# Three projection units instead of two in the staged beginning of a hybrid SSD/Conformer layer, with its first loads and casts in another order

## The chip, the cores and the metric

The kernel runs on one core of a Trainium2 chip, in one launch. Time is device time in microseconds (us): the median of several runs of the same program. The engines are named as in the profile: PE (TensorE, the matrix engine; PEld is its weight load), DVE (VectorE), ACT (ScalarE), POOL (GpSimd) and SP (SyncE, which here issues every DMA). All data are float32; the large products use the type fp32r, which PE runs at one pass.

## What is computed

One layer of a diffusion backbone, for 512 latent tokens (L) and 128 context tokens (C), 640 columns in all (T), with a model width of 1024 (eight blocks of 128, KD). Cut to what the beginning computes:

```python
mod = jax.nn.silu(cond) @ prm["w_ada"] + prm["b_ada"]
sh1, sc1, g1, sh2, sc2, g2 = [m[:, None, :] for m in jnp.split(mod, 6, axis=-1)]
h = rms_norm(x, prm["norm_mix_pre"]) * (1 + sc1) + sh1
proj = h @ prm["w_in"]
z, xbc, dt_raw, cf_in = jnp.split(proj, [...], axis=-1)
xbc = jax.nn.silu(dwconv1d(xbc, prm["w_ssd_conv"], prm["b_ssd_conv"]))
xs, b_mat, c_mat = jnp.split(xbc, [...], axis=-1)
# SSD scan forward and backward over chunks of 128 tokens with dt, a, xs, b_mat, c_mat
cf_a, cf_g = jnp.split(cf_in, 2, axis=-1)
u = dwconv1d(cf_a * jax.nn.sigmoid(cf_g), prm["w_cf_conv"], prm["b_cf_conv"])   # 31 taps
# then layer norm, output projection, residual, gated ConvFFN, residual
```

The modulation (`cond @ w_ada`) differs between latent and context tokens, so two rows of it are computed.

## The kernel before, in words

**Layout.** Features lie on the 128 partitions, tokens along the free axis. x is eight tiles of 128 x 640 (T0 to T7). A *unit* is a projection's weight block: 128 output features, 1024 x 128 weights, a DMA of 512 KB. To keep float32 accuracy each weight and each h is split into a high and a low part: ACT copies to fp32r (L165 for weights, L253 for h), then POOL (L167) or DVE (L255) subtracts. A product is then three matmuls (high by high, high by low, low by high), each in two column parts of 384 and 256, so one k block of a unit is six matmuls and a whole unit 48 (`mm3`, L268).

**Weight buffers.** `fetch` (L133) loads raw units into tag `wr`, which has two buffers; `split_unit` splits them into `wh` and `wl`, which have three each. `get_unit(i)` fetches up to two units ahead. A third raw unit can be loaded only when the splits of the first are done with its buffer.

**Beginning.** SP issues the loads: the condition vectors, x, constants, the first block of modulation weights (`load_ada(0)`, eight DMAs of 256 KB, tag order at L97), all parameters (`prms`, 920 columns), the root table `ids` (a repeated 32 x 32 identity), the dt weights `wdts`. ACT computes Silu of the condition (L345), a one-element square root to have its table loaded (L347), and the squares of x (L351); PE sums them over features (`colsum`, L326); ACT and DVE take the reciprocal root (L340, L341); PE spreads it to all partitions (`spread`, L334).

**Staged part (L365 to L396).** The units in `FIRST`, g0 and a0 (gate and value of the Conformer branch), go on by stages rather than one after the other. x is multiplied by the spread root: four tiles on DVE straight from PSUM (L373) and four on POOL (L375) from a copy that ACT makes (L370). Then, for each of four stages s: `ada_first` multiplies one 2 MB block of modulation weights (L294; SP loads blocks 1 to 3 at L367), turns the result (L276) and adds its bias (L285); DVE forms the scale (L380, L381), applies scale and shift to x blocks 2s and 2s+1 (L385); ACT and DVE split them (L253, L255); PE does the dt product (L360) and the two blocks of every unit in `FIRST`.

**After it.** `gate` (L700, Tanh) and `gated` (L705) make the Conformer input; `dtprep` (L448 on) the dt and decay tables, beginning with a cast of `ids` (L452), a transposing product (L458), and using the exponential of `a_log` (L479); `conv31` the 31-tap convolution, one DVE instruction a tap (L721), accumulating in PSUM tile P2, its first step on ACT (L718). Then the list `seq` is worked through: units B0, C0, xs0, g1, ... each with `proj` (PSUM tiles P0 and P1 in turn) and its consumer; for B0 and C0 that is `conv3_silu` (L417 on ACT, L419 and L421 on DVE, L428 Silu). `ssd` builds decays for each head pair and casts selectors from `ids` (L608). Four steps scale parameters by 0.5 on POOL (L771, L773).

**Order.** The program is built with `schedule_with_timeline_sim=True`. Each engine's instruction order is then not the order of the Python text: a planner simulates a timeline and gives each engine, of the instructions that are ready in its model, the one that is first in the text; `tc.high_priority(offset=-3000)` puts `conv31` behind the rest. `tc.issue_after(ins)` adds an order edge: what it encloses is queued behind `ins` on the engine of `ins`. Once built, each engine runs its queue strictly in order.

Of the kernel before, what the change touches and what calls it, by code (L numbers as in the profile page):

```python
# [7 lines left out]
F32 = mybir.dt.float32  # L8
F32R = mybir.dt.float32r
AF = mybir.ActivationFunctionType  # L10
# [3 lines left out]
P = 128  # L14
# [3 lines left out]
T = L + C  # L18
# [29 lines left out]
def hybrid_layer_kernel(ctx: ExitStack, tc: tile.TileContext, xT, ct, prm, cst, wrest, wdt, idhl_d, wada1, wada2, win,  # L48
# [51 lines left out]

    load_ada(0)
    prms = sb.tile([P, NPRM], F32, tag="prms", name="prms")
    sy.dma_start(prms, prm)
    ids = sb.tile([P, 32], F32, tag="idhl", name="ids")
    sy.dma_start(ids, idhl_d)
    wdts = sb.tile([P, KD, 32], F32, tag="DTW", name="wdts")
    sy.dma_start(wdts, wdt)
    ones = sb.tile([P, 1], F32, tag="ones", name="ones")
# [37 lines left out]
    def get_unit(i):  # L146
        fetch(i + AHEAD)
        return ready.pop(i)
# [29 lines left out]
    IN_INDEX = _in_index()  # L178
    FIRST = ("g0", "a0")
    plan_in(*FIRST)  # L180
    seq = []

    def s_proj(*names):
        for n in names:
            plan_in(n)
            seq.append(("proj", n))

    s_proj("B0", "C0")
    seq += [("btok", 0), ("cb", 0)]
# [57 lines left out]

    split_ins = [None]
    EARLY = 16

    def split_act(hi_tag, lo_tag, src, lo_eng):
        hi = slot(hi_tag, F32R)
        ac.activation(hi, src, AF.Copy)  # L253
        lo = slot(lo_tag, F32R)
        split_ins[0] = lo_eng.tensor_tensor(lo, src, hi.bitcast(F32), SUB)  # L255
        return hi, lo
# [87 lines left out]

    ac.activation(cts, cts, AF.Silu)  # L345

    ac.activation(sb.tile([P, 1], F32, tag="warm", name="warm"), epsc, AF.Sqrt)  # L347
    pst = psq(1)
# [15 lines left out]
    h_hi, h_lo = [], []  # L364
    firsts = [(get_unit(unit_of[n][0]), psum((0, 2, 1)[i])) for i, n in enumerate(FIRST)]  # L365
    for s in range(1, 4):
        load_ada(s)  # L367
    ada_first(0)
    rs0 = slot("S12")
    ac.activation(rs0, prs[:, 192:192 + T], AF.Copy)  # L370
    for k in range(KD):
        if k < 4:
            ve.tensor_tensor(xs_[k], xs_[k], prs[:, 192:192 + T], MUL)  # L373
        else:
            gp.tensor_tensor(xs_[k], xs_[k], rs0, MUL)  # L375
    for s in range(4):
# [37 lines left out]
    def conv3_silu(pt, i, out):  # L414
# [12 lines left out]
        else:  # L427
            ac.activation(out, out, AF.Silu)  # L428

    ACM = DT = acHL = WD = CDs = idr = None  # L430
    cT = [None, None]
# [16 lines left out]
    def dtprep():  # L448

        nonlocal ACM, DT, acHL, WD, CDs, idr  # L450
        idr = sb.tile([P, 32], F32R, tag="idr", name="idr")
        ve.tensor_copy(idr, ids)  # L452
        raw = slot("T8")
# [24 lines left out]
        aexp = sb.tile([P, 32], F32, tag="aexp", name="aexp")  # L478
        ac.activation(aexp, prm_col("a_log", 0, 32), AF.Exp)  # L479
        ve.scalar_tensor_tensor(by(e), DT, -1.0, aexp.unsqueeze(1).to_broadcast([P, NCH, 32]), MUL, MUL)  # L480
# [111 lines left out]
    def ssd(p):  # L592
# [12 lines left out]
        def decays():  # L605
            peas = []
            sel = sm.tile([P, 2, 2, 64], F32R, tag="sel", name=nm("sel"), bufs=1)
            ve.tensor_copy(sel, ids.rearrange("p (d h) -> p d h", d=2)[:, :, 2 * p:2 * p + 2]  # L608
                           .unsqueeze(3).to_broadcast([P, 2, 2, 64]))
            for d in range(2):  # L610
                pea = psq(d)
                te.matmul(pea[:, 0:L], sel[:, d].rearrange("p h q -> p (h q)"), acHL[:, 0:L], start=True, stop=True)
                ea.append(slot(f"S{10 + d}"))
                peas.append(pea)
            for o, pea in zip(ea, peas):
                ac.activation(o[:, 0:L], pea[:, 0:L], AF.Exp)
# [157 lines left out]
    gate(0, firsts[0][1])  # L774
    gated(0, firsts[1][1])
    dtprep()
    conv31(0)
# [684 lines left out]
```

## Time and profile before

| | |
|---|---|
| Median of 3 runs | 1012.25 us (1012.11 to 1014.71) |
| Profiled execution, its own time | 1010.71 us |
| Span of its instructions | 1008.9 us |
| Mean granted PE clock over the span | 0.993 |
| HBM read / written | 97.87 MB / 3.67 MB |
| Chain that ended last, shares | PE 81%, DVE 7%, ACT 5%, POOL 3%, issue 2%, DMA 2% |

How to read the lines quoted below. A *timeline* row is: start in us from the span's beginning, time in us until the end of the last of the merged instructions, engine, line of the kernel, operation, output tile <- input tiles, shapes, count; in brackets how long the engine was idle before it and what released it ("issue": nothing that the profile shows). Matmul counts are hardware instructions: a float32 product outside fp32r takes two. Matmul ends are modelled, so a row's time can overlap the next one's start. A *windows* row is: the stretch, its length, then busy us and instruction count of PE, PEld, DVE, ACT and POOL, the granted PE clock (1.00 is full), the busy share of the DMA engines and GB/s. A *waits* row is: engine and line, what it waited for, us in total, times, longest. A row of *DMA issues* ends with KB each and the median us from issue to landing. SPq is SP's queue of DMA issues.

### The profile page before, as it was taken

What the parts mean: (1) busy time and instruction counts of PE and PEld (TensorE: products, weight loads), DVE (VectorE), ACT (ScalarE), POOL (GpSimd) and SP (SyncE); (2) the same over time, 40 slices, a digit from 0 to 9 for tenths busy, and PEclk for the clock granted to TensorE, in tenths of its full rate; (3) what the DMA queues carried; (4) which work ended last, traced back from release to release, by engine and by line L of the source; (5) the groups of instructions that cost most, each with busy time, mean ns of one, the idle gap of its engine ahead of it and who ended that gap; (6) DMA issues with size and microseconds to landing.
All of it is one profiled execution on the core that took longest, in us unless ns stands there. A gap on an engine that the chain in (4) does not pass through costs nothing.

```text
span 1008.9 us, 18834 instructions
## 1 busy us (share of the span) xinstructions
PE 968.3 (96%) x7655; PEld 933.7 (93%) x7655; DVE 736.1 (73%) x1093; ACT 457.9 (45%) x766; POOL 588.8 (58%) x426
## 2 busy tenths in 40 slices
PE   4999999999999989999989999999999999999995
PEld 2789999999999978899979999999999999999995
DVE  3789999989999998672286798998988988400004
ACT  6244556674553856842364754233233236322211
POOL 2333877888887896443473696454454456543444
PEclk9999999999999999999999999999999999999998
DMA  9622121122212111559463422222222222222212
GB/s 345 229 80 79 53 94 63 54 74 64 74 43 66 41 50 41 167 165 391 156 206 106 147 84 64 85 70 77 85 71 76 84 70 68 79 79 74 79 37 105
DMA packets 42934, 102.76 MB, mean 102 GB/s; under 512 B 4832, under 2 KB 12768, under 8 KB 42848
## 3 DMA queue, kind: packets, MB, share of 16 engines
q1 hardware_dynamic: 42848, 101.56, 30.4%
q8 instruction: 60, 0.98, 0.4%
q14 instruction: 26, 0.21, 0.1%
HBM read 97.87 MB, written 3.67 MB: 101 GB/s over the span
## 4 chain that ended last, share of the span: by engine, by line
PE 81%; DVE 7%; ACT 5%; POOL 3%; issue 2%; DMA 2%; SPq 0%; POOLq 0%; ACTq 0%; DVEq 0%
PE ps L268 67%; PE ps L1112 3%; PE pq L268 2%; POOL wl L167 2%; PE pq L313 2%; PE pq L666 1%; DVE T L760 1%; ACT wh L165 1%; DVE ps L721 1%; PE pq L655 1%; PE pq L573 1%; DMA wr<-in_wout 1%; PE pq L294 1%; PE pq L631 1%; DMA T<-in_xT 1%
## 5 line engine op out<-in xcount | busy, mean ns | idle before, releaser
L167 POOL TENSOR_TENSOR wl<-wr,wh 128x1024 fp32r<-128x1024 f32 (+3 forms) x127 | 291.7, 2297 | 293.3 <-ACT wh L165 287.4
L268 PE MATMUL ps<-H,wh 128*128 128x384 f32 (+1 forms) x1636 | 322.1, 310 | 4.9 <-DVE M L421 2.2
L165 ACT ACTIVATE wh<-wr 128x1024 fp32r<-128x1024 f32 (+3 forms) x131 | 131.7, 1006 | 342.6 <-PE ps L268 196.8
L268 PE MATMUL ps<-T,wh 128*128 128x384 f32 (+1 forms) x1472 | 273.1, 306 | 1.9 <-ACT S L1080 1.9
L268 PEld LDWEIGHTS ps<-H,wh 128*128 128x128 f32 x1636 | 249.0, 188 | 9.1 <-issue 4.5
L1090 DVE SCALAR_TENSOR_TENSOR S<-ps,prms,S 128x441 f32<-128x441 f32 (+2 forms) x336 | 233.4, 695 | 29.7 <-ACT S L1080 19.2
L268 PEld LDWEIGHTS ps<-T,wh 128*128 128x128 f32 x1472 | 219.3, 188 | 2.3 <-ACT S L1080 2.2
L721 DVE SCALAR_TENSOR_TENSOR ps<-u,prms,ps 128x655 f32<-128x655 f32 x223 | 200.7, 900 | 9.9 <-ACT ps L718 5.4
L268 PE MATMUL ps<-H,wl 128*128 128x384 f32 (+1 forms) x818 | 194.8, 310 | 0.0
L268 PE MATMUL ps<-T,wl 128*128 128x384 f32 (+1 forms) x736 | 166.7, 306 | 0.0
L268 PEld LDWEIGHTS ps<-H,wl 128*128 128x128 f32 x818 | 128.8, 188 | 1.6 <-issue 1.2
L268 PEld LDWEIGHTS ps<-T,wl 128*128 128x128 f32 x736 | 113.0, 188 | 0.0
L341 DVE RECIPROCAL rsm<-rsm 128x160 f32<-128x160 f32 (+2 forms) x9 | 7.3, 815 | 141.5 <-ACT rsm L340 141.5
L268 PE MATMUL ps<-S,wh 128*128 128x384 f32 (+1 forms) x420 | 87.5, 312 | 1.7 <-DVE M L923 1.2
L268 PEld LDWEIGHTS ps<-S,wh 128*128 128x128 f32 x420 | 65.9, 188 | 4.3 <-issue 2.5
L268 PE MATMUL ps<-S,wl 128*128 128x384 f32 (+1 forms) x210 | 54.4, 308 | 0.3 <-POOL wl L167 0.3
L637 ACT ACTIVATE S<-pq,ACM 128x128 f32<-128x128 f32 x140 | 40.9, 372 | 18.3 <-PE pq L631 18.1
L1080 ACT ACTIVATE S<-ps,prms 128x640 f32<-128x640 f32 x42 | 36.5, 868 | 0.0
L268 PEld LDWEIGHTS ps<-S,wl 128*128 128x128 f32 x210 | 35.0, 188 | 0.5 <-POOL wl L167 0.5
L588 POOL TENSOR_TENSOR S<-S,stmp 128x128 f32<-128x128 f32 x36 | 18.6, 517 | 15.1 <-ACT S L577 11.2
L1193 POOL TENSOR_TENSOR H<-S,S 128x640 f32<-128x640 f32 x16 | 25.2, 1578 | 0.0
L648 POOL TENSOR_TENSOR S<-S,M 128x640 f32<-128x640 f32 x14 | 22.1, 1577 | 4.4 <-ACT S L645 4.4
(353 smaller groups left out, 1276.7 us busy)
## 6 DMA issues: line engine op xcount, KB each, us to landing
wr<-in_wup SPq DMA_DIRECT2D x44, 512.0 KB, 3.4
wr<-in_win SPq DMA_DIRECT2D x36, 512.0 KB, 3.5
T<-in_wada SPq DMA_DIRECT2D x49, 256.0 KB, 5.4
wr<-in_wdown SPq DMA_DIRECT2D x16, 512.0 KB, 3.4
wr<-in_wout SPq DMA_DIRECT2D x13, 512.0 KB, 3.4
H<-in_wada SPq DMA_DIRECT2D x23, 256.0 KB, 5.5
S<-in_wada SPq DMA_DIRECT2D x16, 256.0 KB, 5.9
wr<-in_wdown SPq DMA_DIRECT2D x8, 384.0 KB, 3.1
```

The source lines that it names most:

```text
L165: ac.activation(hi[:, :n], raw[:, :n], AF.Copy)
L167: lo_eng.tensor_tensor(lo[:, :n], raw[:, :n], hi[:, :n].bitcast(F32), SUB)
L268: last_mm[0] = te.matmul(out, w, x[:, c0:c1], start=first and i == 0, stop=last and i == 2)
L313: te.matmul(pt[32 * j:32 * j + 32, 0:P], cts[:, kc, :], w[:, j * P:(j + 1) * P], start=kc == 0, stop=kc == KD - 1, tile_position=(0, 32 * j))
L588: gp.tensor_tensor(now, now, tmp, ADD)
L637: ac.activation(r[:, c * P:(c + 1) * P], pb[:, (c - c0) * P:(c - c0 + 1) * P], AF.Relu, scale=-1.0, bias=ACM[:, c, row:row + 1])
L648: (ve if i % 2 or last else gp).tensor_tensor(r, r, cbm[g][d], MUL)
L721: ve.scalar_tensor_tensor(acc, u[:, j:j + UO], w(j), acc, MUL, ADD)
L1080: ac.activation(out, v, AF.Identity, bias=prm_col("ffn_b", i), scale=w(1, 1))
L1090: ve.scalar_tensor_tensor(ob, vl[:, r0 + a - 1:r1 + a - 1, q0 + b - 1:q1 + b - 1], w(a, b), ob, MUL, ADD)
L1112: te.matmul(pt[:, o:o + c1 - c0], w[k] if i in (1, 2) else w[:, k * P:(k + 1) * P], x[:, c0:c1], start=k == 0 and j == 0, stop=k == KD - 1 ...
L1193: gp.tensor_tensor(f_raw[q], a, b, MUL)
```

## The change

- `FIRST` gets a third unit: g0, a0 and B0 go by stages. B0 leaves `seq`; its PSUM tile is P1, and since `proj` goes on alternating from P0, C0 now takes P0, xs0 P1 and so on. B0's convolution `conv3_silu` is written behind `gated(0)` and ahead of `dtprep`. In the text its weights are taken with `get_unit` behind the scaling of x.
- Loads: behind the first modulation block come only the first 56 columns of `prms` (modulation bias and the first norm's gain), then g0 and a0, then `wdts`, the second modulation block, the other 864 columns of `prms`, `ids`, and the other two modulation blocks.
- x is scaled on DVE alone, all eight tiles from PSUM; ACT's copy L370 is gone.
- ACT's one-element square root is queued behind the Silu of the condition, not ahead of it.
- Queued later: the cast of `ids` behind the last low split of h on DVE, the selector cast of `decays` behind that cast, the exponential of `a_log` behind the last high split of h on ACT.

PE's products, the weight splits and the bytes loaded stay the same; the one `prms` load becomes two.

```diff
     load_ada(0)
+
     prms = sb.tile([P, NPRM], F32, tag="prms", name="prms")
-    sy.dma_start(prms, prm)
-    ids = sb.tile([P, 32], F32, tag="idhl", name="ids")
-    sy.dma_start(ids, idhl_d)
-    wdts = sb.tile([P, KD, 32], F32, tag="DTW", name="wdts")
-    sy.dma_start(wdts, wdt)
+    NEAR = _COLS["g_mix_pre"][1]
+    sy.dma_start(prms[:, 0:NEAR], prm[:, 0:NEAR])
...
-    FIRST = ("g0", "a0")
+    FIRST = ("g0", "a0", "B0")
...
-    s_proj("B0", "C0")
+    s_proj("C0")
...
-        ac.activation(hi, src, AF.Copy)
+        hi_ins[0] = ac.activation(hi, src, AF.Copy)
...
-    ac.activation(cts, cts, AF.Silu)
-
-    ac.activation(sb.tile([P, 1], F32, tag="warm", name="warm"), epsc, AF.Sqrt)
+    cond = ac.activation(cts, cts, AF.Silu)
+
+    with tc.issue_after(cond.ins):
+        ac.activation(sb.tile([P, 1], F32, tag="warm", name="warm"), epsc, AF.Sqrt)
...
-    firsts = [(get_unit(unit_of[n][0]), psum((0, 2, 1)[i])) for i, n in enumerate(FIRST)]
-    for s in range(1, 4):
+    firsts = [(get_unit(unit_of[n][0]), psum((0, 2)[i])) for i, n in enumerate(FIRST[:2])]
+    wdts = sb.tile([P, KD, 32], F32, tag="DTW", name="wdts")
+    sy.dma_start(wdts, wdt)
+    load_ada(1)
+    sy.dma_start(prms[:, NEAR:], prm[:, NEAR:])
+    ids = sb.tile([P, 32], F32, tag="idhl", name="ids")
+    sy.dma_start(ids, idhl_d)
+    for s in range(2, 4):
         load_ada(s)
     ada_first(0)
-    rs0 = slot("S12")
-    ac.activation(rs0, prs[:, 192:192 + T], AF.Copy)
     for k in range(KD):
-        if k < 4:
-            ve.tensor_tensor(xs_[k], xs_[k], prs[:, 192:192 + T], MUL)
-        else:
-            gp.tensor_tensor(xs_[k], xs_[k], rs0, MUL)
+        ve.tensor_tensor(xs_[k], xs_[k], prs[:, 192:192 + T], MUL)
+    firsts.append((get_unit(unit_of[FIRST[2]][0]), psum(1)))
...
-        ve.tensor_copy(idr, ids)
+        with tc.issue_after(split_ins[0].ins):
+            late = ve.tensor_copy(idr, ids)
+        first_cast.append(late)
...
-        ac.activation(aexp, prm_col("a_log", 0, 32), AF.Exp)
+        with tc.issue_after(hi_ins[0].ins):
+            ac.activation(aexp, prm_col("a_log", 0, 32), AF.Exp)
...
-            ve.tensor_copy(sel, ids.rearrange("p (d h) -> p d h", d=2)[:, :, 2 * p:2 * p + 2]
-                           .unsqueeze(3).to_broadcast([P, 2, 2, 64]))
+            with tc.issue_after(first_cast[0].ins):
+                ve.tensor_copy(sel, ids.rearrange("p (d h) -> p d h", d=2)[:, :, 2 * p:2 * p + 2]
+                               .unsqueeze(3).to_broadcast([P, 2, 2, 64]))
...
     gate(0, firsts[0][1])
     gated(0, firsts[1][1])
+    bT[0] = slot("M2")
+    conv3_silu(firsts[2][1], 8, bT[0])
     dtprep()
```

More of the change, by code (lines that the diff above doesn't have):

```diff
@@ L248, in hybrid_layer_kernel @@
     split_ins = [None]
+    hi_ins = [None]
     EARLY = 16
@@ L428, in conv3_silu @@
             ac.activation(out, out, AF.Silu)
+    first_cast = []
     ACM = DT = acHL = WD = CDs = idr = None
```

## The prediction, made before the changed kernel was built

> **What bounds the kernel now.** I read the page first, then the windows of the first 75 us and of the long middle, then the timeline of each engine at the beginning, then the waits.
>
> ```profile
> PE 968.3 (96%) x7655; PEld 933.7 (93%) x7655; DVE 736.1 (73%) x1093; ACT 457.9 (45%) x766; POOL 588.8 (58%) x426
> 20.00:25.00 5.00, 0.33 (x1) 0.14 (x1) 4.93 (x10) 2.37 (x4) 5.00 (x6) 0.79 1.05 392
> 25.00:35.00 10.00, 9.37 (x92) 6.50 (x93) 7.48 (x6) 1.75 (x3) 6.79 (x5) 0.76 1.05 387
> 35.00:50.00 15.00, 14.16 (x204) 11.74 (x204) 11.23 (x28) 4.92 (x8) 2.77 (x2) 1.00 0.35 128
> 75.00:80.00 5.00, 5.00 (x36) 5.00 (x34) 4.34 (x9) 1.91 (x3) 2.33 (x1) 1.00 0.31 99
> ```
>
> PE is busy for 968.3 of 1008.9 us, and the change adds no matmul and takes none away. So the time can fall only where PE stands idle or runs at a low clock: about 40 us in all. At the beginning that is the stretch 20 to 25 us (0.33 of 5 us busy), the low clock in 25 to 35 us (0.76 of full speed), and 0.84 us in 35 to 50. A full-clock stretch runs 36 products in 5 us, 0.139 us each: one unit of 48 products costs PE 6.7 us, a quarter of it (one stage) 1.7 us.
>
> The PE timeline says what it waits for:
>
> ```profile
> 9.09 4.08 PE L326 MATMUL pq<-S,ones 128*32 128x160 f32 x40 [1.35 <-ACT S L351]
> 15.31 2.50 PE L334 MATMUL ps<-rsm,csts 128*128 128x160 f32 x8 [0.54 <-DVE rsm L341]
> 17.74 2.13 PE L294 MATMUL pq<-T,cts 128*32 128x128 f32 x40
> 20.31 0.33 PE L276 MATMUL pq<-csts,adar 128*128 128x128 f32 x1 [0.44 <-ACT adar L297]
> 25.63 1.03 PE L360 MATMUL pq<-T,wdts 128*32 128x512 f32 x1 [4.99 <-issue]
> 42.20 1.52 PE L294 MATMUL pq<-T,cts 128*32 128x128 f32 x48
> 71.94 0.84 PE L268 MATMUL ps<-H,wh 128*128 128x384 f32 x4 [2.25 <-DVE M L421]
> ```
>
> After the transpose of the first modulation (L276) PE stands still for 4.99 us until the first dt product (L360), which needs x scaled and shifted. And at 71.94 the unit xs0 has waited 2.25 us for L421: B0's convolution on DVE still reads the PSUM tile that xs0 is to fill.
>
> **The change, part by part.** First what leads to that first dt product.
>
> ```profile
> 12.38 1.28 ACT L340 ACT_TABLE_LOAD   x1
> 13.67 0.39 ACT L340 ACTIVATE rsm<-pq,epsc 128x160 f32<-128x160 f32 x1
> 18.58 3.01 DVE L373 TENSOR_TENSOR T<-T,ps 128x640 f32<-128x640 f32 x4 [3.33 <-ACT S L370]
> 21.65 1.69 DVE L608 CAST sel<-ids 128x256 fp32r<-128x256 f32 x1
> 23.26 0.21 DVE L285 TENSOR_TENSOR modv<-pq,prms 128x4 f32<-128x4 f32 x2
> 23.44 1.31 DVE L380 TENSOR_SCALAR asc<-modv 128x4 f32<-128x4 f32 x1
> 35.52 0.17 DVE L380 TENSOR_SCALAR asc<-modv 128x4 f32<-128x4 f32 x1
> 24.98 1.65 DVE L385 TENSOR_SCALAR T<-T,asc,modv 128x512 f32<-128x512 f32 x4
> 18.63 6.10 POOL L375 TENSOR_TENSOR T<-T,S 128x640 f32<-128x640 f32 x4 [17.39 <-ACT S L370]
> ```
>
> *Square-root table.* The root's table is loaded first and thrown out by Silu, so L340 loads it again at 12.38. Behind Silu it stays in. But the root also needs the column sums, which end at 13.17 (9.09 + 4.08). So the step comes at 13.2 and not 13.67: 0.5 us, not 1.28; the range is 0.3 to 1.28. The Trainium skill, "ScalarE: Activation LUTs", section "What ACT_TABLE_LOAD costs", gives about 2.66 us a switch, 1.28 of it the load and the rest a drain. Here the load takes 1.28 us and the root follows 0.01 us behind it, so no drain stands in the trace; by the page's sum the step would still be held by the column sums.
>
> *Scaling.* DVE began 0.77 us after the spread had ended (15.31 + 2.50 = 17.81), since it waited for ACT's copy L370. The copy is gone. The scaling then starts at about 17.3 and takes 8 x 0.75 (3.01 / 4) = 6.0 us on DVE, to 23.3; the two modv additions (0.21) bring it to 23.5. Now L380 begins at 23.44, since two casts (L452, L608; 1.69 us for the larger) are in the way; they go behind the last split. These parts cancel: +0.1 us. What remains is L380's own length: 1.31 us here and 0.17 in a later stage. It ended when POOL's L375 ended (18.63 + 6.10 = 24.73), so it waited for POOL. Without L375, POOL is free for the splits of g0 and a0, which then run in this same stretch. If L380 falls between two of them the step gains 1.1 us; if it falls at the start of one it loses up to 1.3 (a split is 2.41 us, below). I take -0.4 together with the table.
>
> *Weights ahead of most parameters.* The queue's rows:
>
> ```profile
> 12.75 0.33 SPq L103 DMA_DIRECT2D prms<-in_prm  x1
> 14.77 1.01 SPq L141 DMA_DIRECT2D wr<-in_win  x2
> 16.11 6.13 SPq L98 DMA_DIRECT2D S<-in_wada  x8
> 34.83 48.47 SPq L141 DMA_DIRECT2D wr<-in_win  x8
> 20.65 1.06 ACT L165 ACTIVATE wh<-wr 128x1024 fp32r<-128x1024 f32 x1 [0.40 <-DMA wr<-in_win]
> 26.53 5.26 POOL L167 TENSOR_TENSOR wl<-wr,wh 128x1024 fp32r<-128x1024 f32 x2
> 46.44 2.41 POOL L167 TENSOR_TENSOR wl<-wr,wh 128x1024 fp32r<-128x1024 f32 x1 [2.71 <-ACT wh L165]
> 26.59 5.88 DVE L255 TENSOR_TENSOR H<-T,H 128x640 fp32r<-128x640 f32 x2
> 37.54 1.56 DVE L255 TENSOR_TENSOR H<-T,H 128x640 fp32r<-128x640 f32 x2
> ```
>
> Three issues (parameters, root table, dt weights) stood ahead of the weights. The parameters become 56 of 920 columns, the dt weights come right behind g0 and a0, and the rest of the parameters and the table behind the second ada block. The queues moved 392 GB/s in 20 to 25 us, so 0.59 MB less (864 columns of 512 B, the table's 16 KB, the dt weights' 128 KB) ahead of g0 brings it 1.5 us earlier, and the second ada block about 1.2 us (the dt weights still stand ahead of that one). That block's products (64 records; 48 took 1.52 us at full clock, so 2.03 us) now run behind 25.63. With their data earlier and the scaling on DVE longer, more of them should be planned into the 4.99 us gap: I take 40 of 64, -1.2 us, with 0 and -2.0 as ends.
>
> *Splits.* POOL's two weight splits began only at 26.53, behind the scaling. DVE's two splits of h took 5.88 us beside them and 1.56 alone: PE got the low halves of stage 0 late. Now the weight splits end at about 25 (weights at 19.1, then 1.06 and two times 2.41), before DVE's. PE's loss there: 92 records in 9.37 us, where 24 products (3.3), 64 ada records (2.0) and four dt records (0.9 together, under the 1.03 of the first, since they overlap) make 6.2 at full clock, and the clock of 0.76 explains 2.4; 0.8 is left. I take -0.8 (0 to -0.8).
>
> *Three units by stages.* B0 moves 12 products (1.7 us) into each stage. In 35 to 50 us PE idles 0.84 us, which this can fill: -0.4 (0 to -0.8). The real gain is at 71.94:
>
> ```profile
> 64.15 0.87 ACT L417 ACTIVATE M<-ps,prms 128x640 f32<-128x640 f32 x1
> 68.84 0.99 DVE L419 SCALAR_TENSOR_TENSOR M<-ps,prms,M 128x511 f32<-128x511 f32 x2
> 70.80 0.99 DVE L421 SCALAR_TENSOR_TENSOR M<-ps,prms,M 128x511 f32<-128x511 f32 x2
> 71.87 1.28 ACT L428 ACT_TABLE_LOAD   x1 [6.85 <-DVE M L421]
> 55.61 0.89 DVE L705 SCALAR_TENSOR_TENSOR u<-u,ps 128x512 f32<-128x512 f32 x2 [3.80 <-ACT u L700]
> ```
>
> B0's convolution stands between the dt chain and the taps of the first long convolution and is done only at 71.8. In the changed kernel it is written ahead of both, and PSUM tile 1 (B0's) is needed by xs0 only after the whole of C0, 6.7 us later. Its own work is 0.87 + 0.99 + 0.99 us. So the wait of 2.25 us goes: -2.2. What is late next is C0's convolution in front of g1; if that waits as long, this term is 0.
>
> *At nothing:* the aexp and sel steps queued later (ACT idles 6.85 us around 65 to 72, the cover; without it one table load of 1.28 us), the prms rest (needed by the taps' scale only behind stage 3).
>
> Sum for PE at xs0: -0.4 - 1.2 - 0.8 - 0.4 - 2.2 = **-5.0 us**, with ends +1.3 and -7.5.
>
> **Whether it lasts.** PE runs on almost without a stop from there; at 345 us a chain on DVE sets the time.
>
> ```profile
> 56.00:294.00 238.00, 232.94 (x1728) 229.55 (x1727) 225.51 (x302) 130.42 (x251) 176.98 (x148) 1.00 0.21 68
> 345.00:430.00 85.00, 78.86 (x657) 70.50 (x656) 70.45 (x85) 61.14 (x107) 59.03 (x51) 1.00 0.25 82
> DVE ps L721 <- ACT ps L718: 5.4, 4, 1.8
> 358.40 1.97 PE L666 MATMUL pq<-S,S 128*64 128x128 f32 x32 [2.37 <-DVE S L657]
> ```
>
> At 358.40 PE waits for DVE, and it idles 6.1 us in 345 to 430. So DVE must come earlier too. DVE's long work begins at 55.61, when stage 3 of a0 is out. In the changed kernel that is 2.8 us earlier by the terms ahead of it, but three stages of B0 (5.0 us) come first: +2.2 us. To arrive 5.0 us earlier at 294 DVE must close 7.2 us of idle time. It has 12.5 (238.0 - 225.5), of which 5.4 is the wait for each long convolution's first step (L718 on ACT), which stays. 7.1 is left: just enough, and some of it will not close. I take 0.8 off: **-4.2 us**. The profiled execution lasted 1010.71 us (span 1008.9 and 1.8 around it), which gives 1006.5 there; the median of the timed runs is 1.54 us above it, so 1012.25 - 4.2 = **1008.0 us**.
>
> **The rivals.**
>
> *DVE eats it.* Half of the 7.2 us doesn't close: -5.0 + 3.6 = -1.4 us, 1010.9. For it: DVE is 95% busy from 56 to 294 (225.5 / 238), and it starts its long work later. Against it: in those 238 us PE idles only 5.1 us, 2.25 of them at 71.94, so DVE keeps up with PE.
>
> *PE waits for B0's weights: slower.*
>
> ```profile
> wr<-in_win SPq DMA_DIRECT2D x36, 512.0 KB, 3.5
> ```
>
> The raw weights have two buffers, so B0's load waits for the split of g0; and it stood in the queue behind all ada blocks, at 34.83. There it lands near 38.6 (the profile's page has 3.5 us from issue to landing, the row above), and the halves take 1.06 and 2.4: 42.1. If PE's order has B0's stage 0 ahead of the next stage, PE has nothing left at 25.2 + 5.0 (the 6.2 above less 1.2) + 2.4 (low clock) + 2.0 (the third ada block) = 34.6. It idles 7.5 us and then runs at half clock again for as long as now behind 25.63 (10 x 0.24 x 2 = 4.8 us at half clock from 25.0 on, 4.2 of them behind 25.63, 2.1 us lost): -5.0 + 7.5 + 2.1 = +4.6, 1016.9. It decides once the load is issued later than about 28 us. Against it: the split of g0 now ends some 6 us sooner, so the load can be issued ahead of the last ada block.
>
> *The clock stays up.* If the ada products keep PE busy in the gap, the 2.1 us that the low clock costs behind 25.63 go too: -4.2 - 2.1 = -6.3, 1006.0. The clock's row falls to 0.79 in 20 to 25 and stays at 0.76 on average for ten more. The Trainium skill, "TensorE: Matmul & The Clock Gate", Part 1, says that an idle window of about 3.4 us halves the clock and that the windows run free of the kernel; the trace agrees (a gap of 4.99 us, then the low clock), and by that rule a gap cut to 2 us would keep it, while scattered short products may not.
>
> *It isn't done by stages.* The planner puts B0 behind stage 3 as now, because its weights are late, but nothing waits for them. Then DVE starts 2.8 us earlier and all of the 5.0 lasts: 1007.2.
>
> **How the numbers follow.** A measurement here can tell about 0.3%, 3.0 us: faster is below 1009.2, slower above 1015.3. Chances: the forecast 0.42 (its own range 1005.5 to 1010.0), DVE eats it 0.20, late B0 weights 0.14, clock 0.12, not by stages 0.12. Faster: 0.34 + 0.02 + 0 + 0.11 + 0.11 = 0.58. Slower: 0.12 of late weights and 0.02 of a planner's new order further on: 0.14. Same: 0.28. Range: 1004.5 leaves about 0.08 below (the clock together with a full hold), 1014.5 about 0.12 above: 80%.
>
> **What would show it.** Right: no table load at the root, L373 eight times from about 17.3 us, ada records in the gap before the first dt product, L255 at 1.56 us in stage 0, no wait of PE on L421 ahead of xs0, C0 ended near 65 us. Wrong: a PE wait on wl in the first stages; the second L141 group on the queue still behind all ada blocks with PE idle; PE's idle time in 345 to 430 grown by as much as the beginning won.

## The result, and the profile after

The changed kernel takes 1030.24 us (median of 4 runs, 1028.77 to 1030.71), the kernel before 1012.58 in the same comparison (4 runs, 1012.11 to 1014.71). The ratio is 1.0168, 95% interval [1.0149, 1.0186]: slower by about 17 us. The forecast was 1008.0 with a range of 1004.5 to 1014.5, so the sign was wrong. The profiled execution took 1028.77 us, its span 1027.0 (1008.9 before).

From here line numbers are those of the kernel that is spoken of. Those of the changed kernel differ a little: L376 is the scaling (L373 before), L382 the scale's first step (L380), L254 the low split of h (L255), L267 the products (L268), L463 the dt transposes (L458), L638 the decay matmuls (L631), L728 the taps (L721), L755 the gate z's product (L748). A "product" in the tables is one record of L267 (L268), counted from 0 in order of its start. "First decay" and "last decay" are the starts of ACT's first and last instruction that makes a decay (L637 before, L644 after), just behind PE's decay matmul; "DT" is the start of the instruction that writes the tile of dt values, and the taps are those of the long convolutions.

The first row of the page and the windows of the stretches that the prediction spoke of, after; columns as before:

```profile
PE 976.6 (95%) x7655; PEld 939.8 (92%) x7655; DVE 718.7 (70%) x1097; ACT 458.1 (45%) x766; POOL 580.1 (56%) x422
20.00:25.00 5.00, 2.26 (x33) 1.10 (x32) 4.93 (x8) 1.06 (x1) 4.32 (x2) 0.50 1.06 393
25.00:35.00 10.00, 9.45 (x97) 6.72 (x101) 3.87 (x12) 1.73 (x3) 1.64 (x4) 0.74 1.05 390
56.00:294.00 238.00, 230.41 (x1717) 226.56 (x1715) 212.44 (x299) 132.65 (x251) 174.96 (x148) 0.99 0.21 68
345.00:430.00 85.00, 73.26 (x589) 63.73 (x588) 69.28 (x92) 59.72 (x110) 53.02 (x49) 0.90 0.15 47
368.17:385.24 17.07, 11.02 (x36) 7.36 (x37) 13.31 (x19) 12.98 (x36) 13.42 (x14) 0.50 0.00 0
```

PE has the same 7655 instructions and 8.3 us more busy time (976.6 against 968.3), with a mean clock of 0.980 (0.993 before). Its idle time grew by 9.8 us, from 40.6 to 50.4 of the span. Most of it lies late: in 345 to 430 us PE idles 11.7 us (6.1 before) at a mean clock of 0.90 (1.00 before), and one stretch of 17.07 us runs at half clock throughout. DVE, 225.5 us busy from 56 to 294 before, is busy for 212.4 there: it stood idle longer, not shorter.

Because PE's products are the same in number, the start of the n-th product says where time is won and lost:

| product number | before, us | after, us | difference |
|---|---|---|---|
| 192 (first of xs0) | 71.94 | 68.80 | -3.1 |
| 384 | 103.56 | 97.05 | -6.5 |
| 1632 | 334.64 | 339.81 | +5.2 |
| 2304 | 491.99 | 508.63 | +16.6 |
| 4416 | 847.92 | 864.88 | +17.0 |
| 5376 | 990.55 | 1008.68 | +18.1 |

So the beginning did win, and part of the win was kept until about 250 us. There are three losses behind it: some 12 us between products 384 and 1632, another 11 between 1632 and 2304 (340 to 509 us), and 1.2 between the last two rows.

**The beginning after.** Timelines of DVE and PE:

```profile
15.99 5.94 DVE L376 TENSOR_TENSOR T<-T,ps 128x640 f32<-128x640 f32 x8 [1.45 <-PE ps L333]
22.04 2.32 DVE L382 TENSOR_SCALAR asc<-modv 128x4 f32<-128x4 f32 x1
26.19 1.56 DVE L254 TENSOR_TENSOR H<-T,H 128x640 fp32r<-128x640 f32 x2
58.57 0.89 DVE L712 SCALAR_TENSOR_TENSOR u<-u,ps 128x512 f32<-128x512 f32 x2 [5.99 <-ACT u L707]
66.32 0.33 DVE L468 TENSOR_TENSOR T<-pq,prms 128x160 f32<-128x160 f32 x1 [0.52 <-PE pq L463]
89.07 0.31 DVE L482 SCALAR_TENSOR_TENSOR DT<-T 128x160 f32<-128x160 f32 x1
```

```profile
22.17 2.14 PE L293 MATMUL pq<-S,cts 128*32 128x128 f32 x32 [2.05 <-DVE modv L284]
25.19 1.06 PE L360 MATMUL pq<-T,wdts 128*32 128x512 f32 x1 [0.87 <-DVE T L387]
59.93 0.65 PE L360 MATMUL pq<-T,wdts 128*32 128x128 f32 x16
65.09 1.20 PE L463 MATMUL pq<-ids,T 128*128 128x32 f32 x10
```

The same three steps of the dt chain before, from the timelines of PE and DVE:

```profile
49.18 1.99 PE L360 MATMUL pq<-T,wdts 128*32 128x128 f32 x20
54.64 1.20 PE L458 MATMUL pq<-ids,T 128*128 128x32 f32 x10
80.39 0.32 DVE L477 SCALAR_TENSOR_TENSOR DT<-T 128x160 f32<-128x160 f32 x1
```

The steps up to the split are of the kind predicted: eight scalings on DVE, 32 ada records ahead of the first dt product, the split at its undisturbed 1.56 us. But g0 and a0 are complete 3.0 us later (L712 at 58.57, before L705 at 55.61). And the small dt products of the context tokens, which ran at 49.18, now stand behind the last stage of all three units, at 59.93. DT is there 8.7 us later, and the first decay starts at 123.44 us instead of 118.10.

**The late loss.** PE's timeline between the last decays, before and after:

```profile
360.30 0.84 PE L268 MATMUL ps<-H,wh 128*128 128x384 f32 x4
...
366.94 0.87 PE L268 MATMUL ps<-H,wh 128*128 128x384 f32 x4 [0.88 <-ACT T L858]
```

```profile
366.27 0.65 PE L638 MATMUL pq<-HL,idr 128*128 128x384 f32 x2 [1.40 <-DVE T L678]
...
372.16 0.58 PE L638 MATMUL pq<-HL,idr 128*128 128x256 f32 x1 [0.45 <-ACT S L644]
376.17 0.69 PE L638 MATMUL ps<-HL,idr 128*128 128x384 f32 x1 [3.44 <-DVE M L755]
...
387.35 0.85 PE L267 MATMUL ps<-H,wh 128*128 128x384 f32 x4
```

Before, PE has products to fill the pauses between these decays from 360.30 on: the output projection's first part, which the kernel computes ahead of time (`ahead_parts`). After, the first of them comes at 387.35, and from 366.27 on PE has no product at all for 21 us. The row at 376.17 shows the tile that holds it up: the decays of the last head pair wait 3.44 us for DVE's L755, the product that reads the last gate, z7, out of PSUM. The last pair's decays are written to `psum(2 * d)`, tiles P0 and P2, and the ahead parts to `psum(0)`. `proj` alternates P0, P1, P0, ... ; with B0 taken out of it, z7 is its 33rd tile and not its 34th, so z7 lies on P0, which both need.

### The profile page after: what moved, and what is told of

Same layout as the page of the kernel before. It is cut to its first block, busy times and chain, and to the rows that moved or that the text cites. A ratio compares the mean times of both kernels' runs of the same rounds, so it can differ in the third digit from the quotient of the medians.

```text
span 1027.0 us, 18820 instructions
## 1 busy us (share of the span) xinstructions
PE 976.6 (95%) x7655; PEld 939.8 (92%) x7655; DVE 718.7 (70%) x1097; ACT 458.1 (45%) x766; POOL 580.1 (56%) x422
## 4 chain that ended last, share of the span: by engine, by line
PE 83%; DVE 7%; ACT 4%; POOL 2%; DMA 2%; issue 1%; SPq 0%; POOLq 0%; ACTq 0%; DVEq 0%
PE ps L267 69%; PE ps L1121 3%; DVE ps L728 2%; PE pq L267 2%; PE pq L312 2%; PE pq L673 1%; PE pq L662 1%; DVE T L767 1%; ACT wh L163 1%; POOL wl L165 1%; PE pq L579 1%; PE pq L293 1%; DMA T<-in_wada 1%; DVE M L1019 1%; PE pq L638 1%
## 5 line engine op out<-in xcount | busy, mean ns | idle before, releaser
L267 PE MATMUL ps<-H,wh 128*128 128x384 f32 (+1 forms) x1636 | 323.1, 312 | 2.5 <-ACT u L707 1.9
L267 PE MATMUL ps<-T,wh 128*128 128x384 f32 (+1 forms) x1472 | 273.3, 306 | 1.9 <-ACT S L1089 1.9
L267 PEld LDWEIGHTS ps<-H,wh 128*128 128x128 f32 x1636 | 250.9, 190 | 8.6 <-issue 3.9
L267 PEld LDWEIGHTS ps<-T,wh 128*128 128x128 f32 x1472 | 219.3, 188 | 2.3 <-ACT S L1089 2.2
L728 DVE SCALAR_TENSOR_TENSOR ps<-u,prms,ps 128x655 f32<-128x655 f32 x223 | 200.9, 901 | 9.0 <-ACT ps L725 4.4
L267 PE MATMUL ps<-H,wl 128*128 128x384 f32 (+1 forms) x818 | 196.1, 311 | 0.0
L267 PE MATMUL ps<-T,wl 128*128 128x384 f32 (+1 forms) x736 | 166.8, 306 | 0.0
L267 PEld LDWEIGHTS ps<-H,wl 128*128 128x128 f32 x818 | 129.9, 189 | 0.7 <-issue 0.4
L267 PEld LDWEIGHTS ps<-T,wl 128*128 128x128 f32 x736 | 113.0, 188 | 0.0
L267 PE MATMUL ps<-S,wh 128*128 128x384 f32 (+1 forms) x420 | 87.3, 312 | 1.2 <-DVE M L932 1.2
L267 PEld LDWEIGHTS ps<-S,wh 128*128 128x128 f32 x420 | 65.9, 188 | 3.1 <-issue 2.5
L267 PE MATMUL ps<-S,wl 128*128 128x384 f32 (+1 forms) x210 | 54.4, 309 | 0.3 <-POOL wl L165 0.3
L644 ACT ACTIVATE S<-pq,ACM 128x128 f32<-128x128 f32 x140 | 40.3, 377 | 29.8 <-PE pq L638 29.6
L267 PEld LDWEIGHTS ps<-S,wl 128*128 128x128 f32 x210 | 35.0, 188 | 0.5 <-POOL wl L165 0.5
```

The source lines that it names most:

```text
L267: last_mm[0] = te.matmul(out, w, x[:, c0:c1], start=first and i == 0, stop=last and i == 2)
L644: ac.activation(r[:, c * P:(c + 1) * P], pb[:, (c - c0) * P:(c - c0 + 1) * P], AF.Relu, scale=-1.0, bias=ACM[:, c, row:row + 1])
L728: ve.scalar_tensor_tensor(acc, u[:, j:j + UO], w(j), acc, MUL, ADD)
```

## The experiments

**Which of the two it is.** Theory 1: the tile. Theory 2: the late dt chain, and with it the scan. Three kernels separate them. Each ratio is to the kernel before as measured beside that kernel, so ratios can be compared from kernel to kernel better than times.

`e1_tiles`: the changed kernel, with P0 and P1 exchanged in all that follows the projections.

```diff
-                    pbl = psum(2 * d)
+                    pbl = psum((1, 2)[d])
...
-        pm = psum(1)
+        pm = psum(0)
...
-        pr = psum(1)
+        pr = psum(0)
...
-            pt = psum(2 if m in (5, 7) else 0)
+            pt = psum(2 if m in (5, 7) else 1)
...
-        return psum(rot[0] % 3)
+        return psum((1, 0, 2)[rot[0] % 3])
```

> The changed kernel with the names of PSUM tiles P0 and P1 exchanged in everything behind the projections (the last head pair's decays, the layer norm's sums, the ahead parts, the output tiles), so that the last projection z7 again has its own tile, as before the change. Theory 'tile parity' (one projection fewer in the list puts z7 into the tile that the last pair's decays and the ahead parts need, so PE has no filler while DVE is the bound at 350 to 390 us): the loss of 17 us goes, and the time is that of before less what the beginning won, 1003 to 1013 us; ahead products stand between the decay products from about 360 us on. Rival 'late dt chain' (the dt tables come 10 us later, so the scan chain is late and PE starves): stays at 1022 to 1031. Rival 'planner noise' (any new order): anywhere, not within 3 us of the first.

Measured: 1022.12 us, ratio 1.0119 [1.0091, 1.0147]: 5 of the 17 us came back by the two ratios, 8 by the spans of the two profiles (1027.0 and 1018.6 us), in either case fewer than theory 1 alone gives. In its PE timeline the first ahead product starts at 366.31 and none waits for z7:

```profile
366.31 0.85 PE L267 MATMUL ps<-H,wh 128*128 128x384 f32 x4
345.00:430.00 85.00, 78.25 (x646) 70.02 (x645) 70.41 (x86) 59.02 (x109) 58.76 (x52) 0.98 0.21 65
```

PE is busy 78.25 us of 85 there again (78.86 before). But the first decay is as late as in the changed kernel (124.10 us), and the loss up to product 1632 stays (338.86 us, 4.2 later than before).

`e2_flip_alone`: the kernel before, with nothing changed but the tile that `proj` begins with.

```diff
-    flip = [0]
+    flip = [1]
```

> The kernel before with one number changed: the alternation of the projections' PSUM tiles begins with P1 and not P0. Nothing else of the change is in it. Theory 'tile parity': 14 to 19 us slower, 1026 to 1032 us, with PE idle between 355 and 390 us as in the changed kernel. Rivals 'late dt chain' and 'loads and casts': within 3 us of before, 1010 to 1015.

Measured: 1024.73 us, ratio 1.0144 [1.0128, 1.016], a little less than expected. The wait is the one of the changed kernel, in a kernel whose beginning is untouched:

```profile
372.03 0.69 PE L631 MATMUL ps<-HL,idr 128*128 128x384 f32 x1 [3.37 <-DVE M L748]
345.00:430.00 85.00, 70.77 (x580) 60.83 (x579) 70.40 (x92) 60.78 (x108) 53.66 (x50) 0.92 0.17 50
```

Its first and last decays start 1.7 and 0.5 us later than before, but product 2304 starts 13.4 us later. So the tile alone costs 14 us in the kernel before, and it moves PE, while the decays hardly move. Theory 1 holds for this part.

`e3_two_units`: the changed kernel with g0 and a0 by stages and B0 back in the list; loads, casts, root table and scaling stay as changed.

```diff
-    FIRST = ("g0", "a0", "B0")
+    FIRST = ("g0", "a0")
...
-    s_proj("C0")
+    s_proj("B0", "C0")
...
-    firsts.append((get_unit(unit_of[FIRST[2]][0]), psum(1)))
...
-    bT[0] = slot("M2")
-    conv3_silu(firsts[2][1], 8, bT[0])
```

> The changed kernel with only g0 and a0 by stages; B0 is a projection of the list again. The loads, the casts, the table and the scaling stay as changed. Theory 'tile parity': z7 is back in its own tile, so no loss, and the early start remains: 1006 to 1012 us. Rival 'loads and casts' (their new order costs the 17 us): 1024 to 1031.

Measured: 1015.19 us, ratio 1.0054 [1.0034, 1.0074]: 3 us above the expected range, slower than before by 0.5%. PE leads the kernel before by 1.0 to 1.4 us until 340 us, and DT comes at 79.38, 1.0 us earlier. So the loads, casts and scaling delay nothing up to there; what this kernel loses, it loses behind product 1632: of the 4.4 us there, 1.5 go with the places of two tiles (below) and 1.7 with a half-clock stretch of 3.4 us at 571 us. The third unit by stages, its tile apart, costs the difference between e1_tiles and this one, 6.9 us.

**Is it the dt chain?** Theory A says that a late DT is what is left of the loss, theory B that it isn't.

`e5_dt_early` and `e6_dt_first` are e1_tiles with the dt work earlier. The first issues the context tokens' dt products at the head of stage 3; the second also puts `dtprep` ahead of B0's last products and its convolution.

```diff
+        if s == 3:
+            dt_ps.append(psq(0))
+            for k in range(KD):
+                dt_last = dt_product(dt_ps[1], k, L, T)
...
-            for k in (k0, k0 + 1):
+            for k in (k0, k0 + 1) if (i, s) != (2, 3) else ():
...
+    dtprep()
+    with tc.issue_after(pd_last[0].ins):
+        (whi, wlo), pt = firsts[2]
+        for k in (6, 7):
+            mm3(pt, whi, wlo, k, h_hi[k], h_lo[k], False, k == KD - 1)
```

The first hunk is in both, the other two are in e6_dt_first alone; `pd_last` is the last dt transpose.

> Built on the exchanged tiles of e1_tiles; the five dt products of the context part are issued at the head of the last stage of the first projections instead of behind them, so the chain that makes dt starts about 3 us earlier (30 of PE's rows). Theory A (what is left of the loss behind the tiles is the dt chain being late by 10 us, carried into the scan): the first decays come 2 to 4 us earlier than in e1_tiles, the scan ends 2 to 4 us earlier, and the time falls from 1022 to about 1018 (1016 to 1020). Theory B (the scan is late because DVE has eight scalings and B0's tap work more ahead of it, not because of the dt chain): the decays may come earlier, the scan's end and the time stay within 1 us of e1_tiles, 1021 to 1024.

> As e5_dt_early, and the dt preparation also stands ahead of B0's last-stage products and of B0's convolution, with PE's dt matmuls ahead of those products (12 more rows earlier). Theory A: decays another 2 to 4 us earlier, time about 1014 (1010 to 1017), and if the whole lateness of the scan goes, it comes within 0.3% of the kernel before. Theory B: 1020 to 1024, as e1_tiles.

`e7_dt_late` is the opposite test in the kernel before: the dt transposes wait for the end of B0's projection.

```diff
+        yield
         pd = psq(0)
         for c in range(NCH):
-            te.matmul(pd[:, c * 32:(c + 1) * 32], raw[:, c * P:(c + 1) * P], ids, start=True, stop=True)
+            with tc.issue_after(last_mm[0].ins):
+                te.matmul(pd[:, c * 32:(c + 1) * 32], raw[:, c * P:(c + 1) * P], ids, start=True, stop=True)
...
-    dtprep()
+    dt_rest = dtprep()
+    next(dt_rest)
...
             pt = proj(n)
+            if n == "B0":
+                next(dt_rest, None)
```

> The kernel before, with one thing put late: the five small dt matmuls (L458 of before) wait until B0's projection has ended, 52 of PE's rows or about 10 us later; nothing else of the beginning is changed, and the two projection tiles keep their order. Theory A: the decays come about 8 us later, the scan ends 4 to 8 us later, the time rises to 1014 to 1018. Theory B: PE has other work until the decays, nothing later moves, 1009 to 1012.

Measured, with times from the traces (us) and the ratio to the kernel before:

| kernel | dt transposes | DT | first tap | first decay | last tap | product 1632 | product 2304 | ratio |
|---|---|---|---|---|---|---|---|---|
| before | 54.64 | 80.39 | 60.05 | 118.10 | 373.38 | 334.64 | 491.99 | |
| e1_tiles | 65.75 | 89.72 | 61.17 | 124.10 | 378.26 | 338.86 | 498.63 | 1.0119 [1.0091, 1.0147] |
| e5_dt_early | 60.69 | 89.91 | 61.57 | 124.71 | 379.12 | 339.46 | 499.53 | 1.0102 [1.0067, 1.0137] |
| e6_dt_first | 59.27 | 85.28 | 63.48 | 122.97 | 378.30 | 338.88 | 498.61 | 1.0076 [1.0046, 1.0106] |
| e7_dt_late | 60.61 | 88.60 | 56.03 | 125.98 | 389.49 | 348.58 | 509.46 | 1.0147 [1.0107, 1.0187] |

e7_dt_late gives the direction. A dt chain that ends 8.2 us later makes the first decay 7.9 us late, and the kernel goes to 1026.91 us: theory A's direction, but well above its 1014 to 1018. The overshoot has a reason that the edit brought along. The transposes come 6.0 us later; the other 2.2 us are DVE's new order, which puts 42 instructions between the chain's first step and DT, not 36. From about 95 us on the planner's order differs on every engine, and the long convolutions begin 4.0 us earlier than before and end 16.1 us later. What the lateness costs without the new order wasn't separated. Where PE loses the time is seen in the windows, before and then e7_dt_late:

```profile
175.00:300.00 125.00, 122.18 (x928) 119.55 (x927) 116.53 (x150) 72.51 (x140) 103.60 (x88) 1.00 0.21 66
```

```profile
175.00:300.00 125.00, 114.11 (x822) 110.79 (x821) 108.69 (x135) 66.10 (x128) 93.94 (x83) 0.95 0.19 58
```

PE leads the kernel before at product 384, by 6.0 us, and then stands idle for 10.9 us of these 125 (2.8 before): the projections that it ran ahead with are now lacking as a filler for the pauses of the scan.

e5_dt_early tested less than it was meant to: the chain started 5.1 us earlier than in e1_tiles and ended at the same time, partly because DVE's order put B0's short convolution, four instructions, between its steps (the taps there are 14 in both). e6_dt_first did bring DT 4.4 us forward, but the first decay only 1.1, the first tap came 2.3 us later, and its ratio is hardly below that of e1_tiles (the intervals overlap). Both times lie where theory B has them. PE still meets empty pauses; in e6_dt_first:

```profile
266.69 1.08 PE L620 MATMUL pq<-HL,sel 128*128 128x512 f32 x2 [2.32 <-ACT S L450]
283.99 2.50 PE L531 MATMUL pq<-M,M 128*128 128x128 f32 x10 [2.09 <-DVE T L679]
250.00:300.00 50.00, 44.36 (x314) 43.21 (x313) 40.69 (x54) 27.67 (x62) 41.52 (x34) 0.93 0.16 48
```

The same window before and in e1_tiles:

```profile
250.00:300.00 50.00, 47.18 (x352) 45.62 (x351) 46.30 (x59) 28.36 (x61) 40.10 (x33) 1.00 0.18 59
```

```profile
250.00:300.00 50.00, 42.87 (x313) 41.45 (x312) 40.77 (x54) 29.05 (x64) 44.38 (x36) 0.97 0.19 59
```

So an edit that only puts the dt chain late is enough to cause such a loss, with the order that the planner then makes (e7_dt_late), and moving the chain forward doesn't cure it with three units. That the late chain causes this part of the loss in the changed kernel is argued, not shown; the rival, the planner's new order of all engines, is left.

**The last 1.2 us.** `e8_places` is e3_two_units with two tiles declared where the kernel before declares them; every DMA is issued where it was.

```diff
     prms = sb.tile([P, NPRM], F32, tag="prms", name="prms")
+    ids = sb.tile([P, 32], F32, tag="idhl", name="ids")
+    wdts = sb.tile([P, KD, 32], F32, tag="DTW", name="wdts")
...
-    wdts = sb.tile([P, KD, 32], F32, tag="DTW", name="wdts")
...
-    ids = sb.tile([P, 32], F32, tag="idhl", name="ids")
```

> e3_two_units (two units by stages; loads, casts, root table and scaling as changed) with the tiles ids and wdts declared where the kernel before declares them, so that their places in SBUF are as before; every DMA is issued where it was. Theory P (the 1.2 us that the last products, number 4416 to 5376, take longer in all changed kernels come from other places of later tiles): the stretch goes back from 143.8 to 142.6 us and the time from 1015.2 to about 1014. Theory Q (it comes from the order of the DMA queues or from work that arrives late): 143.8 us and 1015 stay.

Measured: 1012.48 us, ratio 0.9997 [0.9982, 1.0012]. Products 4416 to 5376 take 143.79 us in e3_two_units and 142.63 here: theory P. The same split goes through all the kernels. The changed one, e1_tiles, e3_two_units, e5_dt_early and e6_dt_first declare the two tiles later and take 143.79 us. Before, e2_flip_alone, e7_dt_late, e8_places and the two kernels below declare them early and take 142.63. It begins a little ahead of this stretch: products 3840 to 4416 take 83.09 us in the five and 82.77 in the six, so that the places cost 1.5 us in all. PE waits for nothing in this stretch in either, so it is the single matmul that is longer; from the groups of 850 to 990 us, e3_two_units and then e8_places:

```profile
L267 PE MATMUL ps<-S,wh 128*128 128x384 f32 (+1 forms) x182 | 35.2, 311 | 0.0
L267 PE MATMUL ps<-H,wh 128*128 128x384 f32 (+1 forms) x180 | 34.5, 310 | 0.0
L267 PE MATMUL ps<-T,wh 128*128 128x384 f32 x208 | 40.6, 313 | 0.0
```

```profile
L269 PE MATMUL ps<-S,wh 128*128 128x384 f32 (+1 forms) x186 | 35.8, 309 | 0.0
L269 PE MATMUL ps<-H,wh 128*128 128x384 f32 (+1 forms) x182 | 34.5, 308 | 0.0
L269 PE MATMUL ps<-T,wh 128*128 128x384 f32 x208 | 40.7, 314 | 0.0
```

A matmul that reads an S or an H tile is about 2 ns longer (311 and 310 against 309 and 308); one that reads a T tile isn't (313 against 314). All engines run the same instructions in the same order in both kernels, so the places of later tiles in SBUF are what differs; which of them matters wasn't tried. The whole time fell by more than these 1.5 us: the two ratios differ by 0.6%, the spans of the two profiles (1011.9 and 1011.3 us) by 0.6 us. Where the rest lies, the profiles don't show.

**Scan first?** If the scan's chain sets the time up to 430 us, DT should come before the taps. `e9_dt_ahead` does this to e8_places, `e10_three_dt_ahead` to e6_dt_first with the two tiles in their old places.

```diff
             for j in range(1, CFK - 1 - n):
-                ve.scalar_tensor_tensor(acc, u[:, j:j + UO], w(j), acc, MUL, ADD)
+                with tc.issue_after(dt_ins[0].ins) if (p, j) == (0, 1) else nullcontext():
+                    ve.scalar_tensor_tensor(acc, u[:, j:j + UO], w(j), acc, MUL, ADD)
```

> e8_places, and the first tap of the first long convolution on DVE waits for DT, so the chain of small dt instructions runs on DVE without taps between its steps; the taps of that convolution start some 8 us later and nothing is left out. Theory A (the scan's chain, which begins with DT, sets the time up to 430 us): DT at about 67 instead of 77.6 us, the first decays 5 to 8 us earlier (about 110 instead of 116.4), the scan's last tail product 3 to 8 us earlier, time 1005 to 1009. Theory B (DVE's work as a whole sets it, whatever its order): the decays may come earlier, the scan's end and the time do not, 1011 to 1014. Theory C (the taps are what is late, so that they must go first): slower, 1015 to 1020.

> e6_dt_first (three units by stages, exchanged tiles, dt preparation ahead of B0's last products), with the same wait of the first tap for DT and with ids and wdts declared where the kernel before has them. Theory A: DT at about 73 instead of 85.3 us, decays near 115, the 8 us that e6_dt_first was late at the end go, and the time is 1008 to 1013, level with the kernel before or just under it. Theory B: 1018 to 1021, less only the 1.2 us of the places. Theory C: 1023 to 1028.

| kernel | DT | first tap | first decay | last decay | last tap | product 1632 | product 2304 | ratio |
|---|---|---|---|---|---|---|---|---|
| before | 80.39 | 60.05 | 118.10 | 378.76 | 373.38 | 334.64 | 491.99 | |
| e8_places | 77.62 | 57.30 | 116.38 | 378.52 | 372.67 | 332.83 | 491.95 | 0.9997 [0.9982, 1.0012] |
| e9_dt_ahead | 65.79 | 66.03 | 113.83 | 381.55 | 382.27 | 338.10 | 502.80 | 1.0086 [1.0074, 1.0098] |
| e10_three_dt_ahead | 73.06 | 73.31 | 113.73 | 374.60 | 379.53 | 330.66 | 499.78 | 1.004 [1.0022, 1.0059] |

Both miss theory A; e10_three_dt_ahead took 1017.03 us, between A and B, e9_dt_ahead 1022.51. In e9_dt_ahead DT comes 11.8 us earlier than in e8_places, but the first decay only 2.6; the taps start 8.7 us later and end 9.6 later, and the kernel loses 0.9%. That is theory C, and a little more than it priced. But PE first falls behind, by 8.3 us, between products 768 and 864 (169 to 194 us), long before either chain ends. e10_three_dt_ahead is the reverse of e1_tiles: its decays end 4.2 us earlier than before, PE leads by 4.0 us at product 1632, and then it loses 11.8 us up to product 2304. The last convolution is late: its last tap by 6.2 us, and the layer norm's first subtraction, which needs it, at 390.63 instead of 382.78. That this is the cause is argued from the times alone; 3.9 of the 11.8 us come only between products 2112 and 2208 (445 to 480 us), where PE runs at half clock for 3.4 us. PE is busy for less of the window behind the subtraction, before and then e10_three_dt_ahead:

```profile
400.00:430.00 30.00, 29.07 (x238) 26.65 (x233) 20.80 (x25) 25.47 (x31) 14.17 (x8) 1.00 0.43 143
```

```profile
400.00:430.00 30.00, 25.41 (x205) 22.42 (x204) 19.02 (x24) 22.85 (x28) 10.25 (x5) 0.94 0.42 136
```

So two chains run on DVE side by side, the decays and the taps, and in the kernel before they end 5 us apart (378.76 and 373.38). Putting off either cost time: dt in e7_dt_late, the taps in e9_dt_ahead. With three units by stages both begin later, dt by 10 us and the taps by a little, and neither order that was tried saves both. Each of these edits also gave the engines another order further on, so that the price of one late chain by itself isn't known.

## Why the prediction was wrong

*The part up to xs0.* Its mechanisms came, its size less so. The first dt product comes at 25.19 instead of 25.63: -0.4, as forecast, though L382 took 2.32 us, its worse case, and the earlier scaling paid for it. 32 ada records moved into the gap, where 40 were taken. The splits took 1.56 us. The wait on L421 is gone: from 20 to 80 us PE's waits are at L275, L293 and L360 alone, not at a product. Yet xs0 starts 3.1 us earlier, not 5.0. Most of what is missing is the clock: the first half-clock stretch is 10.24 us long and was 6.83, which at half a clock makes 1.7 us.

```profile
20.01:30.25 10.24, 7.31 (x73) 3.84 (x72) 7.58 (x13) 2.51 (x3) 5.96 (x6) 0.50 1.05 389
```

The same window before:

```profile
22.90:29.73 6.83, 4.10 (x24) 2.38 (x24) 6.76 (x11) 1.55 (x3) 6.83 (x8) 0.50 1.05 386
```

The rule that the prediction cited from the Trainium skill ("TensorE: Matmul & The Clock Gate", Part 1), windows of about 3.4 us, agrees in the lengths: 6.83, 10.24 and 17.07 are 2, 3 and 5 times 3.41 us. It doesn't agree in that such a window has to be idle: in the 3.41 us up to 20.01 PE is busy for 1.02, and the longest of its pauses there is the one of 2.13 us in the first row, the pause behind it 2.05.

```profile
19.79 0.33 PE L275 MATMUL pq<-csts,adar 128*128 128x128 f32 x1 [2.13 <-ACT adar L296]
22.17 2.14 PE L293 MATMUL pq<-S,cts 128*32 128x128 f32 x32 [2.05 <-DVE modv L284]
```

So a gap cut to 2 us, by which the prediction would have kept the clock, didn't keep it; the low clock came 2.9 us sooner than before. Where page and trace differ, the trace decides.

*"Whether it lasts" is the step that failed.* It asked one question, whether DVE closes 7.2 us of idle time, and took 0.8 us off the 5.0 won: -4.2. The runs showed a loss of 18.1 us in its place. Three things stood outside the step.

1. *The tile.* The text about the change itself says that `proj` goes on alternating, "C0 now takes P0, xs0 P1 and so on". The prediction followed this to xs0 only, where it gave the -2.2, and not to the last unit, where the same flip puts z7 on the tile of the last decays and of the ahead parts. Shown by e1_tiles (5 to 8 us back) and e2_flip_alone (14 us alone).
2. *The dt chain.* The terms counted B0's 5.0 us ahead of DVE's start (+2.2 forecast; L712 came +3.0), but only for g0 and a0. The small dt products and L458 stand on PE's queue behind B0's last stage as well: +10.8 and +10.5 us, DT +8.7. e7_dt_late shows that an edit that delays DT by about this much costs 14 us, with the order that the planner makes behind it. In the changed kernel the share of the late chain can't be set apart from that of the later taps and of the planner's new order; all are in the 6.9 us between e1_tiles and e3_two_units. How this part comes about stays open.
3. *The places* of two tiles, 1.5 us (e8_places). No view of the kernel before could show that.

The argument "in those 238 us PE idles only 5.1 us, 2.25 of them at 71.94, so DVE keeps up with PE" read the wrong thing from a right number. PE is busy there because it has projections to fill with. Its lead grew from 3.1 us at product 192 to 6.5 at product 384 by running such projections sooner, and it was paid for at 250 to 300 us, where PE idles 7.1 us of 50 after (before 2.8).

```profile
250.00:300.00 50.00, 42.88 (x302) 41.50 (x301) 40.63 (x55) 28.46 (x61) 43.61 (x35) 0.93 0.18 59
```

Two slips of the working change nothing: 7.1 us of idle time are not quite enough to close 7.2, and 34.83 + 3.5 is 38.3, not 38.6, which takes 0.3 us off the rival of B0's weights.

*The rivals.* "DVE eats it" had the right place but not the size: it ended at no change. "PE waits for B0's weights" had the right sign and another mechanism: the load came late (issued at 30.22 us, among the last ada block's), but the planner put B0's first two stages together behind the second stage of g0 and a0, from 41.3 us, and no product waited for the weights. "The clock stays up" is refuted by the windows above, "not done by stages" by the small dt products at 59.93, which stand behind all 144 products of the three units. Of the 0.14 for slower, 0.12 belonged to the late weights; only the 0.02 for "a planner's new order further on" lay near what came, and the tile isn't an order. Of the signs of failure named, the third is what came: PE's idle time in 345 to 430 grew, by 5.6 us, and the clock fell with it.

*The sum of the 18.1 us* in the profiled executions: at product 2304 the changed kernel is 16.6 us late, 6.6 of which e1_tiles has too (the third unit by stages), so that 10.0 are the tile's; then 1.5 for the places of the two tiles. At the end e1_tiles is only 8.4 us ahead of the changed kernel (1018.6 against 1027.0), since it runs at half clock for a while near 536 us, where the changed kernel doesn't. Such stretches lie elsewhere in other kernels (at 571 us in e3_two_units), and no step of the change explains this one.

No version here beats the kernel before. e8_places, which keeps the new loads, casts and scaling but two units and the old places, equals it.

## What to carry to other kernels

When a change takes one member out of a rotation of buffers, follow the rotation to its last user: what the shifted tile meets there can cost more than all that is won at the place of the change. Work that keeps a busy engine busy is a stock: here running ahead with it early gained nothing, since the chains that it covers weren't earlier too, so price a new beginning also by when it hands over the first input of each long chain, and not only by how full it makes the matrix engine. Where two chains end within a few microseconds of each other, as here, putting one first can cost as much as it saves. And where a planner orders the instructions, one late input can change the order of all engines behind it: an experiment that moves one step has to be read with the order that it got.

## What the runs showed of the hardware that was not expected

- A small DVE instruction that meets a POOL instruction can last almost as long as that one. L382 has 128 x 4 elements and takes 0.17 us in other stages; here it takes 2.32 us and ends at 24.36, as POOL's second weight split ends (24.32).

```profile
19.65 4.67 POOL L165 TENSOR_TENSOR wl<-wr,wh 128x1024 fp32r<-128x1024 f32 x2 [18.41 <-ACT wh L163]
33.92 0.17 DVE L382 TENSOR_SCALAR asc<-modv 128x4 f32<-128x4 f32 x1
```

  The Trainium skill ("SBUF — State Buffer", Summary: rules for kernel authors) says that of a DVE and a POOL instruction the second one to issue blocks fully until the first is done, if the DVE instruction is in a two-port mode, or has two SBUF inputs while the POOL instruction reads SBUF. The rows agree with the full block: POOL's second split had begun, at 21.98, when L382 did. L382 has one input tile, modv, which leaves the two-port mode; whether it ran in that the rows don't show.
- The place of a tile in SBUF alone changed the rate of 960 products by 0.8% (143.79 against 142.63 us), the same to 0.01 us within the five and within the six kernels that share their places.
- PE went to half clock without having been idle for a whole window: in the changed kernel the 3.41 us ahead of the stretch at 296.49 us have PE busy for 1.56, with one pause of 1.85.
